# Fifty-two more tiles of an input projection formed as seven products per pair of tiles

## The chip, the cores and the metric

The kernel runs on one core of a Trainium2 chip. The metric is the device time of one execution in microseconds. TensorE (PE in the profile) multiplies matrices, and its weight loads have a row of their own (PEld); VectorE is DVE, ScalarE is ACT, GpSimd is POOL, and SyncE (SP) issues most of the DMAs.

## What is computed

The reference is one inference step of a mixer layer for 1024 prompt tokens and 8 sample tokens (1032 columns in the kernel), model width 1024, all in float32. Cut to what matters:

```
h = rmsnorm(x, norm_pre) * (1.0 + scale) + shift            # scale, shift, gate from c
proj = h @ w_in                                             # 1024 -> 10256 columns
hA, cA, bA, zA, qkv, zB, beta_raw, alpha_raw, gA, gB = split(proj)
yA = ((bA * conv3(cA * hA)) * silu(zA)) @ w_out_a           # branch A
q, k, v = split(silu(conv4(qkv)));  q, k = l2norm(q), l2norm(k)
o, S = gated_delta_chunked(q, k, v, beta, g, s0)            # 8 heads, branch B
yB = (rmsnorm(o, onorm_w) * silu(zB)) @ w_out_b
merged = sigmoid(gA) * yA + sigmoid(gB) * yB
y = x + gate * rmsnorm(merged @ w_o, norm_post)
```

The delta rule of a head works on eight chunks of 128 tokens. Per chunk c a triangular inverse U is formed, and the chunks are scanned in order: X = vp - nx * (K^T S), vn = U^T X, S = egl * S + kd^T vn, and the output of the chunk is Q^T S + DA^T vn. Convolution buffers and final states are outputs too.

## The kernel before

**Tiles and numbers.** A projection is made with 128 output columns as the stationary operand and the 1032 tokens as the moving one; one such tile is 128x1032. w_in has 80 tiles: H, C, B, Z of branch A (8 each), Q, K, V and ZB of the 8 heads (8 each), GA and GB (8 each); beta and alpha are a narrow extra tile of 48 stationary columns. Every float32 number is carried as two rounded parts (xh + xl for h, whi + wlo for a weight; ScalarE casts the high part, VectorE subtracts to get the low one), and a product is three matmuls: high x high, high x low, low x high.

**A normal tile** (`run`) goes over three groups of GW = 344 tokens, eight blocks of 128 input channels (k) and the three matmuls: 72 matmuls of 344 columns. Its weights come as one 512 KB block (`wraw`), split in two halves of 128x512.

**A pair as seven products** (`products`) takes two tiles as the columns of a 2x2 block product: the input channels in halves (weights a11, a12 for the even tile, a21, a22 for the odd one) and the tokens in halves of HT = 516. By Winograd's form of Strassen's scheme the four output blocks C11, C12, C21, C22 come from seven products P1 to P7 of half the channels by half the tokens. P1, P2, P3 and P5 use h itself or a first sum, and P6, P7, P4 and P5 use the sums T2, T3, T4 and T1 of h's quarters; weight sums are formed on VectorE. Each product has two halves of PW = 258 tokens x 4 blocks of channels x 3 matmuls, so a pair has 7 x 24 = 168 matmuls of 258 columns. In PSUM a product lies alone; `evacuate` adds it to the tiles (named acc) in SBUF.

**The order.** After the startup (h, modulation, first tile K0) `run` makes 59 tiles head by head (K, Q, V, two gates, ZB), then H, C, B, Z for t = 0 to 2 (SG = 3). At 936 us `products` makes branch A's other twenty tiles, two pairs at a time, with the sums of h written to memory (txs) and read back; `products_b` (1142 to 1224 us) makes w_out_b's eight tiles the same way; w_out_a follows as eight normal tiles (to 1320 us), and then w_o and the end (to 1420.6 us).

**What runs beside.** All else is written as generators, "strands" (`delta_gen` for a head's delta rule, `conv` strands, `gate_gen`, `weight_gen`, `block_gen` and so on). A small clock model in the kernel (`Sched`) says after each group of three matmuls (`slot`) whether a strand's last step would be finished by then with a slack (SLK = 450 ns); if so its next step is issued there. `force` steps strands until a condition holds. Queues are in order per engine, so this fixes most of the order. In `delta_gen`, DB is the strictly lower matrix of each chunk; its 32x32 diagonal blocks go to memory (sA) and come back as At, the T chain (62 small VectorE instructions on Ttmp and Tw) inverts them, the result goes through memory again (sT) and comes back as Tn, VectorE transposes it (Un), and seven TensorE steps with 32x32 and 64x64 blocks (on Qs, Tn, U, DB) build U. The scan follows with three hops per chunk:

```
stt(X, pk[:, 0:C], nx[:, c:c + 1], vp[:, c, :], ALU.mult, ALU.add)
yield
pv = ps_aux()
PE.matmul(pv[:, 0:C], lhsT=U[:, c, :], rhs=X, start=True, stop=True)
vn = bp.tile([P, C], F32, tag="vn", name="vn", bufs=2)
A.copy(out=vn, in_=pv[:, 0:C])
yield
pS = ps_aux()
PE.matmul(pS[:, 0:C], lhsT=kd[:, c, :], rhs=vn, start=True, stop=True)
```

SBUF buffers of tile width come from `Slots` (T4: NT4 = 6 equal ones, more once pools are released); PSUM has four banks for tiles (pm) and four for strands (pa). All instructions are issued through one helper, so nearly all have line L121 (L124 after the change) in the profile, and are told apart by the names of their tiles.

## Time and profile before

| | |
|---|---|
| time, median of 2 runs | 1423.52 us (1422.89 to 1424.15) |
| the profiled execution's own time | 1422.29 us |
| its span, first to last instruction | 1420.6 us |
| mean granted TensorE clock | 0.997 |
| TensorE busy | 1396.6 us (98%), 10130 instructions |
| VectorE busy | 937.7 us (66%), 2444 |
| ScalarE busy | 658.0 us (46%), 1521 |
| DMA | 161.76 MB, 114 GB/s over the span |

The profile is one execution as the hardware recorded it. Busy time counts instructions that compute; waiting, register and DMA-issuing instructions are not in it. The chain is the work that ended last, followed back from the end. A window's row gives each engine's busy time in one stretch, the clock that TensorE was granted there (1.00 is full speed), the DMA engines' busy share and what they moved.

### The profile page before, as it was taken

What the parts mean: (1) busy time and instruction counts of PE and PEld (TensorE: products, weight loads), DVE (VectorE), ACT (ScalarE), POOL (GpSimd) and SP (SyncE); (2) the same over time, 40 slices, a digit from 0 to 9 for tenths busy, and PEclk for the clock granted to TensorE, in tenths of its full rate; (3) what the DMA queues carried; (4) which work ended last, traced back from release to release, by engine and by line L of the source; (5) the groups of instructions that cost most, each with busy time, mean ns of one, the idle gap of its engine ahead of it and who ended that gap; (6) DMA issues with size and microseconds to landing.
All of it is one profiled execution on the core that took longest, in us unless ns stands there. A gap on an engine that the chain in (4) does not pass through costs nothing.

```text
span 1420.6 us, 25886 instructions
## 1 busy us (share of the span) xinstructions
PE 1396.6 (98%) x10130; PEld 1341.2 (94%) x10130; DVE 937.7 (66%) x2444; ACT 658.0 (46%) x1521; POOL 36.5 (3%) x72
## 2 busy tenths in 40 slices
PE   6999999999999999999999999999999999999997
PEld 4899999999999999999999999999999999999786
DVE  6754846758468494494764816978977857864553
ACT  6767453845529465284573332343333344532211
POOL 0000000000001000010000000000000200000000
PEclk9999999999999999999999999999999999999999
DMA  9523352233323333324232323255621875643221
GB/s 321 147 48 94 91 118 71 80 86 93 87 70 106 87 84 94 72 76 106 62 110 69 85 62 86 95 176 170 207 76 31 248 250 182 231 151 93 95 85 59
DMA packets 191396, 161.76 MB, mean 114 GB/s; under 512 B 34311, under 2 KB 166816, under 8 KB 191266
## 3 DMA queue, kind: packets, MB, share of 16 engines
q1 hardware_dynamic: 186720, 151.58, 36.3%
q0 software_dynamic: 4352, 8.46, 2.0%
q8 instruction: 79, 1.29, 0.4%
q14 instruction: 43, 0.35, 0.1%
q10 hardware_dynamic: 202, 0.08, 0.0%
HBM read 123.40 MB, written 36.91 MB: 113 GB/s over the span
## 4 chain that ended last, share of the span: by engine, by line
PE 91%; DVE 5%; DMA 3%; ACT 1%; SPq 0%; issue 0%; DVEq 0%; ACTq 0%
PE pm_t L121 66%; PE pa_t L121 22%; PE pb L121 2%; DVE kq L121 1%; DMA xs<-in_x_prompt_dram 1%; DMA yraw<-yAsc 1%; DMA wor<-in_w_o_dram 0%; DVE S L121 0%; SPq L121 0%; DMA sg<-gAsc 0%; DVE wlo L121 0%; DVE Tw L121 0%; DVE Ttmp L121 0%; DMA sg<-gBsc 0%; DVE ml L121 0%
## 5 line engine op out<-in xcount | busy, mean ns | idle before, releaser
L121 PE MATMUL pm_t<-xh,whi 128*128 128x344 f32 (+1 forms) x1576 | 520.1, 330 | 0.0
L121 PE MATMUL pm_t<-xl,whi 128*128 128x344 f32 (+1 forms) x1576 | 498.1, 316 | 0.0
L121 PE MATMUL pm_t<-xh,wlo 128*128 128x344 f32 (+1 forms) x1576 | 498.1, 316 | 0.0
L121 PEld LDWEIGHTS pm_t<-xh,whi 128*128 128x128 f32 x1576 | 297.0, 188 | 2.0
L121 PEld LDWEIGHTS pm_t<-xl,whi 128*128 128x128 f32 x1576 | 297.0, 188 | 0.2
L121 PEld LDWEIGHTS pm_t<-xh,wlo 128*128 128x128 f32 x1576 | 296.3, 188 | 0.1
L121 DVE TENSOR_TENSOR wlo<-wraw,whi 128x512 fp32r<-128x512 f32 x136 | 92.0, 687 | 49.6 <-ACT whi L121 49.3
L121 ACT CAST whi<-wraw 128x512 fp32r<-128x512 f32 x136 | 82.7, 624 | 75.9 <-PE pm_t L121 73.3
L121 ACT CAST whi<-wr 128x1024 fp32r<-128x1024 f32 x42 | 44.0, 1047 | 84.6 <-PE pm_t L121 40.7
L121 DVE SCALAR_TENSOR_TENSOR kq<-raw,vecs,kq 128x528 f32<-128x528 f32 x96 | 69.2, 761 | 1.9 <-ACT kq L121 1.9
L121 PE MATMUL pm_t<-thi,wlo 128*128 128x258 f32 x240 | 67.9, 283 | 0.1
L121 PE MATMUL pm_t<-thi,whi 128*128 128x258 f32 x240 | 67.7, 282 | 0.0
L121 PE MATMUL pm_t<-tlo,whi 128*128 128x258 f32 x240 | 67.7, 282 | 0.0
L121 PE MATMUL pa_t<-thi,whi 128*128 128x258 f32 x224 | 64.0, 286 | 1.2 <-ACT whi L121 1.2
L121 PE MATMUL pa_t<-thi,wlo 128*128 128x258 f32 x224 | 64.1, 286 | 0.8 <-DVE wlo L121 0.8
L121 PE MATMUL pa_t<-tlo,whi 128*128 128x258 f32 x224 | 63.7, 285 | 0.0
L121 PE MATMUL pm_t<-yhi,whi 128*128 128x344 f32 x192 | 61.5, 321 | 0.0
L121 PE MATMUL pm_t<-ylo,whi 128*128 128x344 f32 x192 | 61.4, 321 | 0.0
L121 PE MATMUL pm_t<-yhi,wlo 128*128 128x344 f32 x192 | 61.3, 320 | 0.0
L121 DVE TENSOR_TENSOR wlo<-wr,whi 128x1024 fp32r<-128x1024 f32 x42 | 51.2, 1219 | 14.5 <-ACT whi L121 14.5
L121 DVE TENSOR_TENSOR Ttmp<-Tw,At 128x60 f32<-128x60 f32 (+24 forms) x248 | 51.9, 209 | 8.8 <-DMA At<-sA 3.7
L121 ACT ACTIVATE junk<-pa_t 128x128 f32<-128x128 f32 x192 | 53.8, 280 | 5.6 <-PE pa_t L121 2.7
(407 smaller groups left out, 2837.2 us busy)
## 6 DMA issues: line engine op xcount, KB each, us to landing
wraw<-in_w_in_dram SPq DMA_DIRECT2D x60, 512.0 KB
wr<-in_w_in_dram SPq DMA_DIRECT2D x40, 256.0 KB
aw<-in_ada_w_dram SPq DMA_DIRECT2D x16, 512.0 KB
gBsc<-gate SPq DMA_DIRECT2D x8, 516.0 KB
gAsc<-gate SPq DMA_DIRECT2D x8, 516.0 KB
txs<-phi SPq DMA_DIRECT2D x8, 516.0 KB
txs<-plo SPq DMA_DIRECT2D x8, 516.0 KB
tlo<-txs POOLq DMA_DIRECT2D x8, 516.0 KB, 8.1
```

Source lines behind the costliest of these rows:

```text
L121: r = f(*args, **kw)
```

## The change

The tiles of x are reordered and mostly paired. Normal are K, Q and V of head 0, one gate tile, and H, C, B, Z of t = 0 (NA0 = 1): eight tiles. The other 72 are 36 pairs: H/C and B/Z of t = 1 to 7, pairs of gates, K/Q of head h, and V of head h with ZB of head h-1. Ahead of the K/Q pair of heads 1 to 7 stand 0, 2, 3, 3, 3, 3, 3 other pairs (FILL). `pairs_run` makes them one pair at a time. Products accumulate in PSUM as far as they share a sign: two tiles pp_t of two banks each ("lanes") take them, and `pair_out` moves a lane with both halves at once, 516 columns wide: four copies on ScalarE and four adds on VectorE per pair. T2, T3, T4 are made once by `block_gen`, stay in SBUF (pool tb), and T1 takes the place of the first channels' second token half in xh and xl after the last normal tile. Weights come as blocks of 128x4x128 (256 KB) in five buffers (`wr`), and splits run at most NWS = 3 products ahead in two strands (`pair_hi`, `pair_lo`).

T4 has fifteen slots of equal width; the heads' K, Q, V, kd, vp, DB, DA, At, Ts, U and gcB, which had buffers of their own, use them (Ts holds Tw, Qs, Tn and Un). Strands have ranks, a step of the lower ranks waits while VectorE or ScalarE are further than LAG1 = 2500 or LAG2 = 600 ns ahead of TensorE in the model (or HOLD = 8000 ns have gone), and the scan's slack is SLS = 200. w_out_a's tiles now come straight after the pairs, with their rows in xh and xl, and `products_b` follows them; the gates of yB are applied by halves, and the tiles of the end go in another order.

On TensorE, where head 0's inverse (on Ts, U, DB) and the start of its scan stand, the kernel before has a group of three matmuls of a normal tile (pm_t) between the steps; two pieces, the first from the inverse, the second from the scan (S,kq to X,U):

```order
L121 MATMUL pa_t<-Qs,Tn 32x32 x8
L121 MATMUL pa_t<-Tn,Qs 32x32 x8
L121 MATMUL pm_t<-xh,whi 128x344
L121 MATMUL pm_t<-xl,whi 128x344
L121 MATMUL pm_t<-xh,wlo 128x344
```

```order
L121 MATMUL pa_t<-S,kq 128x128 x2
L121 MATMUL pa_t<-qs_s,S_2391 128x2 x4
L121 MATMUL pm_t<-xh,whi 128x344
L121 MATMUL pm_t<-xl,whi 128x344
L121 MATMUL pm_t<-xh,wlo 128x344
L121 MATMUL pa_t<-X,U 128x128
```

After the change TensorE has at the same place, in the middle of pair 0 (pp_t are its lanes, T2h and T2l the parts of T2), the following rows:

```order
L124 MATMUL pp_t<-T2h,wlo 128x258
L124 MATMUL pa_t<-Ts,DB 32x32 x16
L124 MATMUL pa_t<-Ts 32x32 x24
L124 MATMUL pa_t<-U,DB 64x64 x8
L124 MATMUL pa_t<-Ts,T_728 64x64 x8
L124 MATMUL pa_t<-vp,U 128x128
L124 MATMUL pa_t<-vn,kd 128x128
L124 MATMUL pa_t<-vn,DA 128x128
L124 MATMUL pa_t<-S,K 128x128
L124 MATMUL pa_t<-S,Q 128x128
L124 MATMUL pa_t<-X,U 128x128
L124 MATMUL pp_t<-T2h,whi 128x258
```

The steps of the inverse and of the first chunk and a half now follow each other with no tile work between them, and pair 0's remaining matmuls stand behind them.

On VectorE, in the scan of head 0, the kernel before has the T chain of head 1 between the scan's rows (S and X):

```order
L121 SCALAR_TENSOR_TENSOR S_2708<-S_2651,egl_96,pa_t_2705 128x128
L121 TENSOR_TENSOR Ttmp_2498<-Tw_2497,At_2496 128x50
L121 TENSOR_TENSOR Tw_2497<-Tw_2497,Ttmp_2498 128x2x25
L121 TENSOR_TENSOR Ttmp_2498<-Tw_2497,At_2496 128x48
L121 TENSOR_TENSOR Tw_2497<-Tw_2497,Ttmp_2498 128x2x24
L121 TENSOR_TENSOR Ttmp_2498<-Tw_2497,At_2496 128x69
L121 SCALAR_TENSOR_TENSOR X_2725<-pa_t_2721,nx_1323,vp_1496 128x128
```

and after the change it has the last sums of h there (qa and qb are sums under way; T2l, T3l, T4l are low parts of the finished ones):

```order
L124 SCALAR_TENSOR_TENSOR X_1972<-pa_t_1968,nx_1364,vp_1295 128x128
L124 TENSOR_TENSOR qb_1966<-qb_1966 128x516
L124 TENSOR_TENSOR T2l_723<-qb_1966,T2h_722 128x516
L124 SCALAR_TENSOR_TENSOR S_1982<-S_1958,egl_96,pa_t_1979 128x128
L124 TENSOR_TENSOR T3l_725<-qa_1965,T3h_724 128x516
L124 SCALAR_TENSOR_TENSOR X_1993<-pa_t_1989,nx_1364,vp_1295 128x128
L124 TENSOR_TENSOR T4l_727<-qb_1966,T4h_726 128x516
L124 SCALAR_TENSOR_TENSOR S_2004<-S_1982,egl_96,pa_t_2001 128x128
```

The sums' last parts, which pair 0's own products need, stand behind rows of the scan's second to fourth step, and the scan's rows behind them.

The diff, cut to its core:

```diff
-NT4 = 6
+NT4 = 15
...
+SLS = 200.0
+LAG1, LAG2 = 2500.0, 600.0
+HOLD = 8000.0
+NWR, NWS = 5, 3
+FILL = (0, 2, 3, 3, 3, 3, 3)
+NA0 = 1
...
-SG = 3
...
+    def due(e):
+        pe = sched.clk["PE"]
+        return max(sched.clk["V"], sched.clk["A"]) <= pe + LAGS[e.pri] or e.t + HOLD <= pe
...
+    PAIRS = []
+    for h in range(1, NH):
+        for _ in range(FILL[h - 1]):
+            PAIRS.append(fill.pop(0))
+        PAIRS.append(((COL_K + h * P, 3), (COL_Q + h * P, 3), lambda a, b, h=h: (k_done(h, a), q_done(h, b))))
+        PAIRS.append(((COL_V + h * P, 3), (COL_ZB + (h - 1) * P, 0), lambda a, b, h=h: (
+            v_done(h, a), z_done(h - 1, b), start(sample_gen(h - 1)))))
...
+    EARLY = ("P4", "P1", "P2", "P6", "P5", "P7", "P3")
...
+    def pair_out(n, p, v, ta, tb):
+        pair = lambda x_: x_.rearrange("p (h n) -> p h n", h=2)
+        C11, C12, C21, C22 = (pair(x_[:, o:o + HT]) for x_ in (ta, tb) for o in (0, HT))
+        copy, adds = {"P1": (C11, ()), "P2": (None, (C11,)), "P6": (C12, ()), "P5": (C22, ()),
+                      "P7": (None, (C22, C21) if order_of(n) is EARLY else (C22,)), "P3": (None, (C12,)),
+                      "P4": (C21, ())}[p]
+        if copy is not None:
+            A.copy(out=copy, in_=v)
+        for out in adds:
+            tt(out, v, out, ALU.add)
+
+    def pairs_run():
+        for n, (e_, o_, done) in enumerate(PAIRS):
+            if n == len(PAIRS) - 2:
+                start(rows_load())
+                start(rows_split())
+            tiles, views = [], []
+            for c0, off in (e_, o_):
+                t_ = T4.take("acc", CW if off else NT, lambda: 4 if any(not h_ or flags.get(("done", h_ - 1)) for h_ in waiting) else 0)
+                if off:
+                    GP.memset(t_[:, 0:off], 0.0)
+                tiles.append(t_)
+                views.append(t_[:, off:off + NT])
+            if n % 2:
+                lanes = [ps_pair(), ps_pair()][::-1]
+            else:
+                lanes = [ps_pair(), ps_pair()]
+            for j, p in enumerate(order_of(n)):
+                blk = {"P6": "T2", "P7": "T3", "P4": "T4", "P5": "T1"}.get(p)
+                force(lambda: (n, p) in made and (blk is None or blk in blocks))
+                unit[0] = 7 * n + j
+                whi, wlo = made.pop((n, p))
+                lane = lanes[LANE.get(p, int(order_of(n) is EARLY))]
+                first = p in ("P1", "P2", "P5") or (p == "P4" and order_of(n) is EARLY)
+                for half in range(2):
+                    ps = lane[:, half, :PW]
+                    for k in range(4):
+                        xh_, xl_ = operand(p, k, half)
+                        PE.matmul(ps, lhsT=whi[:, k, :], rhs=xh_, start=first and k == 0, stop=False,
+                                  skip_group_check=True)
+                        PE.matmul(ps, lhsT=whi[:, k, :], rhs=xl_, start=False, stop=False, skip_group_check=True)
+                        PE.matmul(ps, lhsT=wlo[:, k, :], rhs=xh_, start=False, stop=k == 3, skip_group_check=True)
+                        if k < 3:
+                            slot()
+                    if half == 0:
+                        slot()
+                pair_out(n, p, lane[:, :, :PW], *views)
+                slot()
+            done(*tiles)
...
+    def block_gen():
+        part = lambda v, k: v[:, (k % 2) * HT:(k % 2) * HT + HT]
+        t1 = {}
+        for k in range(4):
+            yield from when(lambda: T4.ready(2 if k % 2 else 3))
+            a, b = T4.get("qa", NT), T4.get("qb", NT)
+            if k % 2 == 0:
+                t1[k // 2] = T4.get("q1", NT)
+            tt(a, xh[:, k, :].bitcast(F32), xl[:, k, :].bitcast(F32), ALU.add)
+            yield
+            tt(b, xh[:, 4 + k, :].bitcast(F32), xl[:, 4 + k, :].bitcast(F32), ALU.add)
+            yield
+            t_ = part(t1[k // 2], k)
+            tt(t_, a[:, HT:NT], a[:, 0:HT], ALU.subtract)
+            tt(a[:, HT:NT], b[:, HT:NT], a[:, HT:NT], ALU.subtract)
+            yield
+            tt(b[:, HT:NT], b[:, HT:NT], t_, ALU.subtract)
+            tt(b[:, 0:HT], b[:, 0:HT], b[:, HT:NT], ALU.subtract)
+            yield
+            for bl, v in (("T2", b[:, HT:NT]), ("T3", a[:, HT:NT]), ("T4", b[:, 0:HT])):
+                hi, lo = (w_[:, k, :] for w_ in T["x", bl])
+                A.copy(out=hi, in_=v)
+                yield
+                tt(lo, v, hi.bitcast(F32), ALU.subtract)
+                yield
+            T4.give(a)
+            T4.give(b)
+        for bl in ("T2", "T3", "T4"):
+            blocks[bl] = T["x", bl]
+        yield from when(lambda: flags.get("normal"))
+        for i in range(2):
+            hi, lo = (x_[:, 2 * i:2 * i + 2, HT:NT] for x_ in (xh, xl))
+            v = t1[i].rearrange("p (k n) -> p k n", k=2)
+            A.copy(out=hi, in_=v)
+            yield
+            tt(lo, v, hi.bitcast(F32), ALU.subtract)
+            T4.give(t1[i])
+            yield
+        blocks["T1"] = True
...
-    run(jobs, 1, isp)
-    products()
+    run(jobs, 1, inx)
+    flags["normal"] = True
+    pairs_run()
...
+    run(jobs, ioa, len(jobs), (ioa,))
+    RS.on = True
     products_b()
-    run(jobs, ioa, len(jobs))
```

More of the change, by code (lines that the diff above doesn't have):

```diff
@@ L719, in drain_bg @@
+            for v in held:
+                T4.give(v)
+            if after:
+                after()
+            slot()
     def drain_bg():
@@ new lines, in hybrid_step, with k_done, q_done, v_done @@
+    heads = [{} for _ in range(NH)]
+    def k_done(h, raw):
+        start(conv_gen(8 + h, raw, "K", lambda d: (heads[h].update(k=d), start(decay_gen(h, heads[h])))))
+    def q_done(h, raw):
+        start(conv_gen(h, raw, "Q", lambda d: heads[h].update(q=d)))
+    def v_done(h, raw):
+        start(conv_gen(16 + h, raw, "V", lambda d: (heads[h].update(v=d), start(delta_gen(h, heads[h])))))
+    def z_done(h, z):
+        def gen():
+            act(z, z, AF.Silu)
+            V.tensor_copy(out=z_s[:, h, :], in_=z[:, S:NT])
+            yield
+            heads[h]["sz"] = z
+        start(gen())
@@ new lines, in gate_done, with gen @@
+    def gate_done(t, sc, g):
+        def gen():
+            store(sc[t], g)
+            T4.give(g)
+            yield
+        start(gen())
+    gc_rows = lambda h: gsc.rearrange("(c h) i -> h c i", h=NH)[h].unsqueeze(0).to_broadcast([P, NC, C])
+    def decay_gen(h, st):
+        yield from when(lambda: flags.get("ba") and (not h or flags.get(("inv", h - 1))), lambda: T4.ready(2))
+        DB_, DA_ = (T4.get(n_, S) for n_ in ("DB", "DA"))
+        DB, DA = (v.rearrange("p (c i) -> p c i", i=C) for v in (DB_, DA_))
+        SY.dma_start(out=DA, in_=gc_rows(h))
@@ new lines, in hybrid_step, with pair_load, pair_split @@
+    praw = {}
+    def pair_load():
+        for n, (e_, o_, _) in enumerate(PAIRS):
+            for part in ("22", "11", "12", "21") if order_of(n) is EARLY else ("11", "12", "21", "22"):
+                c0, half = (e_, o_)[part[0] == "2"][0], int(part[1]) - 1
+                yield from when(wr_ready)
+                praw[n, part] = w_block(w_in, c0, half)
+                yield
+    def pair_split(idx, key, src):
+        yield from when(lambda: unit[0] >= idx - NWS + 1)
+        hi, lo = (wpool.tile([P, 4, P], F32R, tag=t_, name=t_, bufs=NWS) for t_ in ("whi", "wlo"))
+        A.copy(out=hi, in_=src)
+        yield
+        tt(lo, src, hi.bitcast(F32), ALU.subtract)
+        made[key] = (hi, lo)
+        yield
@@ L1471, in yblock_gen @@
             for kk in (0, 2):
+                hi, lo, give = yield from r_pair("yb", p == "P1")
                 if p in ("P1", "P2", "P3"):
[L1473 to L1474 removed]
+                    yield from when(lambda: T4.ready())
+                    raw = T4.get("yraw", NT)
                     k0 = kk if p == "P1" else 4 + kk
@@ L1671, in to_products, with gate_start @@
-    def to_products():
-        drain_bg()
+        gates_left[t] = gates_left.get(t, 2) - 1
+        if not gates_left[t]:
+            T4.give(acc_)
+    gated = {}
+    def gate_start(t, half):
+        gated[t, half] = gate_gen(t, half)
+        start(gated[t, half])
+    def products_b():
+        force(lambda: parked)
         bp.release()
         T4.extend(alloc("m", "left"), "sl", NSL, NT)
-        raw = {}
-        for g in (weight_load(raw), weight_gen(raw), block_gen()):
-            start(g)
@@ L1687, in load_rows, with rows_load, rows_split @@
+    rows = {"ya": {}}
+    yraw = {}
+    def rows_load():
         for k in range(NK):
-            yield from when(lambda: T4.ready(3))
-            raw, hi, lo = (T4.get(n_, NT) for n_ in ("yraw", "yhi", "ylo"))
-            SY.dma_start(out=raw, in_=ysc[k])
+            yield from when(lambda: T4.ready(1 + RES))
+            raw = T4.get("yraw", NT)
+            SY.dma_start(out=raw, in_=yAsc[k])
+            yraw[k] = raw
             yield
-            A.copy(out=hi.bitcast(F32R), in_=raw)
+    def rows_split():
+        for k in range(NK):
+            yield from when(lambda: k in yraw and unit[0] >= 7 * len(PAIRS) - (3 if k < 4 else 1))
+            raw = yraw.pop(k)
+            A.copy(out=xh[:, k, :], in_=raw)
@@ L1809, in prep @@
         n = P if i < 8 else NB
+        for t in range(NK):
+            finish(gated[t, 0 if 0 <= i < 4 else 1])
         xr = S_.get("xr", D)
```

941 lines of the change are left out of this document (473 added, 468 removed).

## The prediction

> **What bounds the kernel now.** I read the page first, then the windows by stage, the chain of waits, the groups by form, and the timeline where the change touches it.
>
> ```profile
> span 1420.6 us, 25886 instructions
> PE 1396.6 (98%) x10130; PEld 1341.2 (94%) x10130; DVE 937.7 (66%) x2444; ACT 658.0 (46%) x1521; POOL 36.5 (3%) x72
> PE 91%; DVE 5%; DMA 3%; ACT 1%; SPq 0%; issue 0%; DVEq 0%; ACTq 0%
> ```
>
> TensorE is busy for 98% of the span and carries 91% of the chain that ended last. So the time is TensorE's work plus the places where it stands. By stages (columns: us, then busy time of PE, PEld, DVE, ACT, POOL with instruction counts, then granted clock, DMA share, GB/s):
>
> ```profile
> 61.00:160.00 99.00, 98.22 (x645) 95.52 (x646) 58.07 (x166) 61.36 (x134) 1.38 (x5) 1.00 0.31 77
> 260.00:360.00 100.00, 99.95 (x757) 98.03 (x756) 73.12 (x227) 62.46 (x162) 3.15 (x7) 1.00 0.32 90
> 936.00:1142.00 206.00, 206.00 (x1722) 205.94 (x1722) 169.92 (x267) 73.70 (x105) 10.29 (x15) 1.00 0.52 159
> 1142.00:1224.00 82.00, 79.94 (x634) 78.28 (x633) 58.24 (x91) 37.73 (x44) 1.29 (x2) 0.98 0.62 204
> 1224.00:1320.00 96.00, 95.76 (x587) 90.99 (x586) 56.42 (x86) 32.97 (x40) 0.00 (x0) 1.00 0.48 155
> 1320.00:1420.60 100.60, 92.92 (x400) 73.73 (x398) 47.37 (x144) 18.34 (x43) 0.00 (x0) 0.98 0.20 69
> ```
>
> From 61 to 1320 us TensorE hardly stops; idle time is at the start and in the last row, which is w_o and which the change leaves nearly as it is. The third row is branch A's twenty tiles as seven products: not 0.01 us of TensorE is lost there, though VectorE works 169.92 of 206 us (82%). In the normal tiles VectorE works 59 to 73%.
>
> What the two kinds of matmul cost is in the chain (start, us, what), where a run of 48 stands without a break, since the durations of single matmuls overlap:
>
> ```profile
> 941.85 5.74 PE pm_t L121 x48
> 1239.29 7.56 PE pm_t L121 x48
> L121 PE MATMUL pm_t<-xh,whi 128*128 128x344 f32 x1416 | 474.9, 335 | 0.0
> L121 PE MATMUL pm_t<-xh,whi 128*128 128x258 f32 x160 | 45.2, 283 | 0.0
> ```
>
> The first run lies in the products: 5.74/48 = 119.6 ns for 258 columns. The second lies in w_out_a: 7.56/48 = 157.5 ns for 344. By width alone the ratio would be 0.75, and it is 0.759, so the narrow matmul loses almost nothing. The group means, 335 and 283 ns, are latencies and must not be summed.
>
> **TensorE's work: -67 us.** Before, 52 tiles of x are normal that belong to pairs afterwards (59 normal tiles and the first against 8 in all; by the instruction order 3744 matmuls of 344 go and 4368 of 258 come). A pair costs 2x72 matmuls of 344, 144 x 157.5 = 22.68 us; as seven products it costs 7x2x4x3 = 168 of 258, 168 x 119.6 = 20.09 us. 26 pairs x 2.59 = **67.3 us**. Everything else on TensorE keeps its count: head strands, w_out_a, w_out_b, w_o.
>
> Now a rule that speaks against the change. The Trainium skill, "TensorE: Matmul & The Clock Gate", section "Back-to-back issue gap", gives for streams of weight load and matmul about 81 ns at 128 columns and 131 ns at 512. Drawn straight between these (an estimate from that page) 258 columns would take 98 ns and 344 would take 109, a pair would rise from 15.7 to 16.4 us, and the 26 pairs would cost some 20 us more instead of 67 less. The two runs of 48 above contradict it: here the time grows by 37.9 ns for 86 columns, 0.44 ns a column, and not by 0.13.
>
> **Work beside it: VectorE, about +5 us.** Per pair it now has seven weight splits and four weight sums of 512, and four adds of 516 out of PSUM; ScalarE has seven casts and four copies.
>
> ```profile
> L121 DVE TENSOR_TENSOR wlo<-wraw,whi 128x512 fp32r<-128x512 f32 x136 | 92.0, 687 | 49.6 <-ACT whi L121 49.3
> L121 ACT CAST whi<-wraw 128x512 fp32r<-128x512 f32 x136 | 82.7, 624 | 75.9 <-PE pm_t L121 73.3 <-PE pa_t L121 1.8 <-ACT U L121 0.7
> L121 DVE TENSOR_TENSOR acc<-pm_t,acc 128x258 f32<-128x258 f32 x68 | 27.5, 420 | 14.9 <-PE pm_t L121 14.9
> L121 DVE SCALAR_TENSOR_TENSOR kq<-raw,vecs,kq 128x528 f32<-128x528 f32 x96 | 69.2, 761 | 1.9 <-ACT kq L121 1.9
> ```
>
> 15 instructions x 0.69 = 10.3 us a pair, against four splits (2.7 us) for two normal tiles; over 26 pairs +197 us. Against that, branch A's products before took fourteen adds of 258 per pair (the 68 of the row, and as many from the other banks, for ten pairs). With all instructions of the order priced this way VectorE goes from 1034 to 1197 us; since the page counts 937.7 where this sum gives 1034, I expect near 1086, 78% of the new span. Spread over 36 pairs it is about 20 us per 23 us of TensorE, strands included, and in some five pairs, where a head's convolution (the rows of 528) and its T chain fall together, it equals TensorE's time. Cover: splits may run two products (5.74 us) ahead, and a PSUM lane has one product of the other lane, 24 x 119.6 ns = 2.87 us, to be evacuated in; an add of 516 takes about 0.69. Lower bound 0: the window 936 to 1142 has the same ratio, 82%, and lost nothing. Upper bound: five pairs that stand 5 us each, 25. I take 5, near the row measured.
>
> **Head 0, first pair: +18 us.** This is where the order changes most. Before, head 0's inverse had 15 us to spare behind its transpose, and 344-column work between its steps:
>
> ```profile
> 135.07 0.60 DVE L121 SCALAR_TENSOR_TENSOR DB<-pa_t,cB,DB 128x128 f32<-128x128 f32 x2
> 147.67 0.19 DVE L121 TENSOR_TENSOR Ttmp<-Tw,At 128x31 f32<-128x31 f32 x1 [3.50 <-DMA At<-sA]
> 159.39 0.23 DVE L121 TENSOR_TENSOR Ttmp<-Tw,At 128x72 f32<-128x72 f32 x1
> 159.66 0.23 DVE L121 TENSOR_TENSOR Tw<-Tw,Ttmp 128x72 f32<-128x72 f32 x1
> 179.81 0.17 DVE L121 TENSOR_TENSOR Tw<-Tw,Ttmp 128x8 f32<-128x8 f32 x1
> 189.60 0.44 DVE L121 STREAM_TRANSPOSE Un<-Tn 128x256 f32<-128x256 f32 x1
> 204.51 0.69 PE L121 MATMUL pa_t<-Un,DB 32*32 32x32 f32 x16
> 205.24 0.36 ACT L121 COPY Qs<-pa_t 32x256 f32<-32x256 f32 x1 [3.22 <-PE pa_t L121]
> ```
>
> The way through memory (DB to At) takes 12 us, one T-chain instruction 0.27, the way back (Tw to Un) up to 9.8, and one step of the inverse 205.60-204.51 = 1.1. In the order of after, only some 32 us of matmuls stand between the last one that DB needs and the inverse, and TensorE's queue is in order: the rest of pair 0 stands behind the inverse, and is itself short of T2, T3, T4, whose last parts VectorE makes between the scan's steps. Working, with head 0's last DB at about 130 (its matmuls stand 5 us earlier in the order than before): At at 142; 62 T instructions of 0.2 to 0.27 (14 us) and nine large ones of 0.6 to 1.1 between them (8 us), to 164; 8 back, 172. TensorE arrives at 161 to 162: **10 us** of waiting. Behind it stand seven inverse steps (8 us) and the scan's first five chunks, with hardly one product's matmul between two hops. A hop:
>
> ```profile
> 305.67 0.38 PE L121 MATMUL pa_t<-vn,kd 128*128 128x128 f32 x2
> 306.09 0.35 DVE L121 SCALAR_TENSOR_TENSOR S<-S,egl,pa_t 128x128 f32<-128x128 f32 x1 [1.17 <-PE pa_t L121]
> 307.07 0.61 PE L121 MATMUL pa_t<-S,kq 128*128 128x128 f32 x4
> 307.49 0.35 DVE L121 SCALAR_TENSOR_TENSOR X<-pa_t,nx,vp 128x128 f32<-128x128 f32 x1 [1.05 <-PE pa_t L121]
> 308.46 0.38 PE L121 MATMUL pa_t<-X,U 128*128 128x128 f32 x2
> 308.88 0.27 ACT L121 COPY vn<-pa_t 128x128 f32<-128x128 f32 x1 [2.03 <-PE pa_t L121]
> ```
>
> 0.77, 0.77 and 0.69 us from a matmul's start to its reader's end, 2.2 a chunk and some 2.4 with the way back to TensorE: five chunks 12, the inverse 8, together 20, in a stretch whose matmuls fill 12.5: **8 us**. Bounds: 10 if the T chain comes 8 us earlier (VectorE's large rows moved less), 28 if the T blocks' last parts come late as well. I take 18. Where cover is gone, each further us on VectorE here is a us of TensorE.
>
> **The other scans: +7.** The same sum of hop needs against the matmuls that stand between, over all 64 chunks, leaves 0.6 us uncovered before and 13 after, six of them in pair 0. Nearest rows: before, 0 us are lost; with every hop bare it would be 56 chunks x about 0.5 = 28. I take 7.
>
> **Transitions: +5.** From w_out_a to w_out_b, which now change places, the row gate, the loads of yB and their splits, the first weights of w_out_b and the sums of yB crowd: about 13.5 us of VectorE by its rows beside 13.5 of TensorE. Before, the like entry cost this:
>
> ```profile
> 1142.39 8.31 DMA yraw<-yAsc
> L121 DVE TENSOR_TENSOR ylo<-yraw,yhi 128x1032 fp32r<-128x1032 f32 x8 | 9.8, 1227 | 4.8 <-ACT yhi L121 4.7
> ```
>
> The window from 1142 shows what was lost in TensorE, 82.00 - 79.94 = 2.1. Bounds 0 and 12 (the 8.31 us transfer bare, and a few splits); I take 5, with the entry to w_out_a. The end stays: the last 7.6 us have no matmul in either order. SP issues more but smaller weight loads (256 KB, twice as many), at 0.31 to 0.52 DMA share; priced at nothing, since a pair of 20 us uses four blocks, five buffers hold 25 us of work, and the longer DMA above takes 8.
>
> **Sum** against the profiled execution's own 1422.29 us (span 1420.6), 1.2 below the median of 1423.52 and inside the runs' spread of 1422.89 to 1424.15 but for 0.6: 1422.3 - 67.3 + 5 + 18 + 7 + 5 = 1390; by the median 1391. The lowest ends of the four stalls (0, 10, 0, 0) give 1365, the upper ones (25, 28, 28, 12) 1448; three of the four values lie nearer to their lower end because the nearest rows do, and I put the forecast at **1388**.
>
> **Rivals.** (a) *Nearly all of the gain arrives*: T chain early, VectorE's 82% harmless as in the products of before; only pair 0's bound of 10 is lost: 1422.3 - 67.3 + 10 = **1365**. For it: the products' 206.00 of 206.00. (b) *VectorE becomes the bound* in the pairs with heads, 25 there: with the rest as above 1355 + 25 + 18 + 7 + 5 = 1410, with the upper ends of the first pair and of the transitions too 1355 + 25 + 28 + 7 + 12 = 1427: **1410 to 1427**, taken at 1412. For it: about 87% mean load with peaks at 100%; against it, queues that even out over a pair. (c) *The slower side*: the evacuation cover of 2.87 us is missed at VectorE's adds, because a lane's next product may not start before the add that stands behind splits and strand work in VectorE's queue. Three such products a pair, 108 in all; from 0.65 us each on (a single split ahead of the add) it eats the 67 us: 108 x 0.65 = 70, **1425 and more without the other terms**, 1450 with them. Against it: the row of 258 adds shows VectorE waiting for TensorE (14.9 us idle), and no group of TensorE waiting for an add. (d) *The narrow matmul does not keep 119.6 ns* once strands and head copies stand beside it: at 135 ns a pair costs 22.68, and all the gain goes, **about 1455** with the stalls above. The skill's rule on the gap would be its reason; the row of 48 stands against it. (e) That it does not do what it says: the counts of the order exclude it.
>
> **How the numbers follow.** Forecast 0.52 (1378 to 1398), (a) 0.23 (1360 to 1378), (b) 0.19, (c) 0.04, (d) 0.02. About 2% is what a measurement of this kernel can tell from no change; 2% below the median is 1395. Faster: (a) and four fifths of the forecast's own case, 0.23 + 0.41 = 0.64. Slower by over 2% (above 1452): 0.03. Same: 0.33. The range of 8 in 10 is 1360 to 1413: it takes in (a) and the lower half of (b).
>
> **What would show it.** Right: matmul steps of 119.6 in the pairs; TensorE idle some 10 us near 162 to 172, released by a DMA of Tn or by VectorE's transpose, and in short pieces to 185; VectorE near 78%; little idle between 200 and 1200. Wrong: TensorE idle at many starts of a product behind VectorE's wlo or acc (b or c), or steps longer than 125 ns (d), or no gap near 165 (a).

## The result and the profile after

The changed kernel takes 1591.15 us (median of two runs, 1585.94 and 1596.37) against 1423.52: **11.8% slower**, ratio 1.1178, 95% interval 1.1019 to 1.1336. The forecast was 1388. The profiled execution took 1596.37 us, the slower of the two. Times are medians of a kernel's executions, without one slow execution of the first kernel under "Earlier heads". The head of its page and the chain by engine:

```profile
span 1594.7 us, 28048 instructions
PE 1427.4 (90%) x10754; PEld 1348.3 (85%) x10754; DVE 1071.9 (67%) x2625; ACT 748.1 (47%) x1655; POOL 44.5 (3%) x144
PE 53%; DVE 18%; DMA 16%; ACT 7%; issue 5%; SPq 1%; POOL 0%; DVEq 0%; ACTq 0%; POOLq 0%
```

TensorE is idle for 167 us of the span, where it was for 24. It is also busy for 31 us longer, although its matmuls should take 67 us less. The windows of after by stage (projections of x, w_out_a, w_out_b, w_o; engines as in the rows of before, then granted clock, DMA share, GB/s) show why:

```profile
61.00:1236.00 1175.00, 1077.36 (x8736) 1044.52 (x8736) 835.82 (x2145) 600.98 (x1423) 27.46 (x108) 0.94 0.29 79
1236.00:1345.00 109.00, 102.64 (x613) 97.71 (x614) 55.68 (x79) 36.96 (x44) 1.29 (x2) 0.97 0.81 265
1345.00:1458.00 113.00, 92.27 (x685) 88.06 (x683) 86.11 (x146) 46.54 (x77) 10.29 (x15) 0.92 0.65 198
1458.00:1587.00 129.00, 106.83 (x416) 79.67 (x416) 46.83 (x136) 18.82 (x44) 0.00 (x0) 0.93 0.15 51
```

The same cuts of before are these (there w_out_b stands ahead of w_out_a):

```profile
61.00:1131.00 1070.00, 1068.61 (x8117) 1048.76 (x8118) 722.53 (x2002) 518.61 (x1314) 22.69 (x35) 1.00 0.35 98
1131.00:1216.00 85.00, 82.94 (x675) 82.31 (x674) 61.55 (x98) 40.74 (x52) 7.89 (x11) 0.98 0.66 215
1216.00:1316.00 100.00, 100.00 (x622) 96.29 (x621) 60.38 (x89) 35.78 (x44) 0.00 (x0) 1.00 0.49 155
1316.00:1413.00 97.00, 96.68 (x416) 75.41 (x414) 47.45 (x137) 19.03 (x44) 0.00 (x0) 1.00 0.22 77
```

So the projections take 105 us more, w_out_b 28, w_out_a 9 and w_o 32: together the 174 us between the two spans. In the projections 98 us are idle time, and the clock of 0.94 means that it stood at half for some 140 us of the 1175, idle time included. The waits of after name the cause (engine and tile <- releaser: us in all, times, longest):

```profile
ACT DA L124 <- DMA DA<-gsc: 42.9, 8, 7.3
ACT L124 <- DMA gcB<-gsc: 34.0, 5, 9.8
ACT gcB L124 <- DMA gcB<-gsc: 12.0, 3, 5.8
PE pp_t L124 <- ACT acc L124: 38.5, 15, 8.5
PE pa_t L124 <- ACT vn L124: 19.2, 7, 5.0
PE pp_t L124 <- DVE ms L124: 15.5, 5, 8.3
ACT sqj L124 <- DMA out_dram<-yt: 30.0, 5, 6.3
```

DA and gcB are the two broadcasts of a head's decay rows, 512 KB each, 16 in all. ScalarE stands 89 us in front of them. TensorE's own largest waits, 38.5 and 19.2 us, are for two of ScalarE's copies: of a lane to acc, and of vn in the scan. Before, one load per head served both; from head 2 on it was issued 16 to 53 us before its first reader (for heads 0 and 1 only 8 and 9 us, with waits of 2.9 and 8.0). Afterwards each of the two goes into a slot of T4, and the sixteen first readers run 8.3 to 11.5 us after the issue. The timeline of after at head 1 shows one such stop from end to end (start, length, engine, operation, idle time before it):

```profile
224.30 0.37 SPq L124 DMA_DIRECT2D DA<-gsc  x1
226.72 0.28 ACT L124 ACTIVATE junk<-pa_t 128x128 f32<-128x128 f32 x1
233.68 0.40 ACT L124 ACTIVATE DA<-DA,ngc 128x128 f32<-128x128 f32 x1 [6.58 <-DMA DA<-gsc]
...
233.75 0.28 PE L124 MATMUL pp_t<-T3h,wlo 128*128 128x258 f32 x1
...
237.06 0.58 ACT L124 COPY acc<-pp_t 128x516 f32<-128x516 f32 x1
237.69 0.39 PE L124 MATMUL pp_t<-xh,whi 128*128 128x258 f32 x1 [3.65 <-ACT acc L124]
```

The load is issued at 224.30 and its first reader runs at 233.68. The copy that frees a PSUM lane (acc) stands behind it in ScalarE's queue, and TensorE waits 3.65 us for the lane. The kernel's clock model had counted 3.3 us from issue to arrival; it is 9.4. Windows of 2 us around a stop at head 2 show what follows one:

```profile
306.00:308.00 2.00, 0.39 (x4) 0.19 (x2) 0.00 (x0) 0.00 (x0) 0.00 (x0) 1.00 0.44 73
308.00:310.00 2.00, 0.00 (x0) 0.00 (x0) 0.00 (x0) 0.00 (x0) 0.00 (x0) 0.94 0.71 170
310.00:312.00 2.00, 0.00 (x0) 0.00 (x0) 0.00 (x0) 1.75 (x2) 0.00 (x0) 0.50 0.64 179
314.00:316.00 2.00, 2.00 (x11) 2.00 (x11) 1.97 (x4) 0.59 (x2) 0.00 (x0) 0.50 0.17 30
318.00:320.00 2.00, 2.00 (x19) 2.00 (x18) 1.97 (x4) 1.97 (x3) 0.00 (x0) 1.00 0.08 23
```

The last matmul ends at 306.4. The clock of 0.94 in the row from 308 to 310 places the change to half near 309.8, some 3.4 us later, and it stays there when work has come back: 11 matmuls from 314 to 316 in place of 19. The Trainium skill, "TensorE: Matmul & The Clock Gate", section "HAM oscillation — how this bites in real kernels", puts the limit at gaps of some 3.4 us. The stop at head 2 fits this, but the trace as a whole does not bear the limit out: in w_o half clock follows a stop of 2.3 us already (1533.2 to 1535.4, for ms), while stops of 1.8 and 2.0 us at 585.5 and 1326.1 have none behind them.

```profile
1533.00:1535.00 2.00, 0.15 (x1) 0.00 (x0) 0.34 (x1) 0.69 (x2) 0.00 (x0) 1.00 0.04 8
1535.00:1537.00 2.00, 1.59 (x4) 1.30 (x5) 0.41 (x2) 0.00 (x0) 0.00 (x0) 0.53 0.00 0
```

### The profile page after: what moved, and what is told of

Its sections match the earlier page's. It is cut to its first block, busy times and chain, and to the rows that moved or that the text cites. A ratio compares the mean times of both kernels' runs of the same rounds, so it can differ in the third digit from the quotient of the medians.

```text
span 1594.7 us, 28048 instructions
## 1 busy us (share of the span) xinstructions
PE 1427.4 (90%) x10754; PEld 1348.3 (85%) x10754; DVE 1071.9 (67%) x2625; ACT 748.1 (47%) x1655; POOL 44.5 (3%) x144
## 4 chain that ended last, share of the span: by engine, by line
PE 53%; DVE 18%; DMA 16%; ACT 7%; issue 5%; SPq 1%; POOL 0%; DVEq 0%; ACTq 0%; POOLq 0%
PE pp_t L124 40%; PE pa_t L124 12%; DMA DA<-gsc 4%; DMA gcB<-gsc 4%; DVE acc L124 3%; DVE wlo L124 3%; DVE Ts L124 2%; DVE Ttmp L124 2%; PE pb L124 1%; DMA sg<-gAsc 1%; ACT junk L124 1%; DVE yt L124 1%; DMA Ts<-sT 1%; ACT DA L124 1%; DVE wr L124 1%
## 5 line engine op out<-in xcount | busy, mean ns | idle before, releaser
L124 PE MATMUL pp_t<-xh,whi 128*128 128x258 f32 (+1 forms) x1624 | 493.8, 305 | 45.0 <-ACT acc L124 18.3
L124 PE MATMUL pp_t<-xl,whi 128*128 128x258 f32 (+1 forms) x1624 | 485.1, 299 | 5.9 <-DVE xl L124 5.9
L124 PE MATMUL pp_t<-xh,wlo 128*128 128x258 f32 (+1 forms) x1624 | 485.9, 300 | 1.3 <-DVE wlo L124 1.3
L124 PEld LDWEIGHTS pp_t<-xh,whi 128*128 128x128 f32 x1624 | 316.8, 195 | 55.2 <-ACT acc L124 20.7
L124 PEld LDWEIGHTS pp_t<-xl,whi 128*128 128x128 f32 x1624 | 317.0, 195 | 6.9 <-DVE xl L124 6.6
L124 PEld LDWEIGHTS pp_t<-xh,wlo 128*128 128x128 f32 x1624 | 316.6, 195 | 3.5 <-DVE wlo L124 2.7
L124 ACT CAST whi<-wr 128x512 fp32r<-128x512 f32 x250 | 153.6, 619 | 233.5 <-PE pp_t L124 192.8
L124 DVE TENSOR_TENSOR wlo<-wr,whi 128x512 fp32r<-128x512 f32 x250 | 170.3, 685 | 67.5 <-ACT whi L124 61.0
L124 DVE TENSOR_TENSOR acc<-pp_t,acc 128x516 f32<-128x516 f32 (+1 forms) x171 | 108.3, 646 | 37.6 <-PE pp_t L124 36.8
L124 ACT COPY acc<-pp_t 128x516 f32<-128x516 f32 (+2 forms) x164 | 92.0, 565 | 39.3 <-PE pp_t L124 34.0
L124 PE MATMUL pp_t<-xh,mh 128*128 128x512 f32 x128 | 55.1, 431 | 25.8 <-DVE ms L124 15.5
```

What stands on the lines that cost most here:

```text
L124: r = f(*args, **kw)
```

## The experiments

Theory A: ScalarE's queue in front of the sixteen loads, and the half clock behind each stop. Theory B: VectorE's and ScalarE's load in the pairs.

**Rows of 4 KB.** In memory the decay rows of one head lay 4 KB apart, eight rows of 512 B. Here they lie together.

```diff
+        gch = small(P, 64)
+        V.tensor_copy(out=gch.rearrange("p (h c) -> p c h", h=NH), in_=gc)
-        transpose(pt[:64, 0:C], gcf)
+        transpose(pt[:64, 0:C], gch)
...
-    gc_rows = lambda h: gsc.rearrange("(c h) i -> h c i", h=NH)[h].unsqueeze(0).to_broadcast([P, NC, C])
+    gc_rows = lambda h: gsc.rearrange("(h c) i -> h (c i)", h=NH)[h].unsqueeze(0).to_broadcast([P, S])
```

> The decay rows of all heads are stored so that one head's eight rows lie together: each of the sixteen broadcast loads (DA and gcB, 512 KB each) reads 4 KB rows in place of 512 B rows; nothing else changes, and the order of instructions stays. Theory A (ScalarE's queue stands in front of these loads, the casts and copies behind it stop TensorE, and each stop is followed by half clock): if the load takes about 3 us less, ScalarE's waits for it fall from 89 us to 40 to 50 and the time falls by 40 to 70 us, to 1520 to 1550. Theory B (VectorE's and ScalarE's load in the pairs sets the time, the waits are a symptom): within 10 us of 1591. If the load itself does not get shorter, the run tells nothing between the two.

Measured: 1504.5 us (1496.7 to 1513.9), 87 less, more than expected. The load at head 1 is now issued at 208.66 and read at 212.36, 3.7 us in place of 9.4. The DMA view of that load, first of after, then of this run:

```profile
DMA packets 1771, 0.91 MB, mean 95 GB/s; under 512 B 33, under 2 KB 1770, under 8 KB 1770
```

```profile
DMA packets 1483, 1.19 MB, mean 221 GB/s; under 512 B 48, under 2 KB 1355, under 8 KB 1483
```

The load has become 128 packets of 4 KB (1483 - 1355) in place of 1024 of 512 B. The waits, TensorE's behind ScalarE among them, and the first stage of this run:

```profile
ACT L124 <- DMA gcB<-gsc: 10.2, 5, 4.9
ACT DA L124 <- DMA DA<-gsc: 6.9, 5, 2.3
ACT gcB L124 <- DMA gcB<-gsc: 0.7, 1, 0.7
PE pp_t L124 <- ACT acc L124: 9.8, 10, 3.3
PE pa_t L124 <- ACT vn L124: 1.4, 4, 0.5
```

```profile
61.00:1138.00 1077.00, 1036.25 (x8736) 1005.09 (x8736) 835.80 (x2146) 601.05 (x1424) 27.43 (x108) 0.98 0.31 86
```

Of ScalarE's 89 us of waits 18 are left, of TensorE's 58 behind ScalarE 11; idle time falls from 98 to 41, and the clock rises to 0.98. ScalarE's and VectorE's busy time is the same to 0.1 us, so B is out as the main cause. The later stages are as long as in after (108, 112, 129 us). The shorter load also lets transfers behind it in the DMA queue come sooner: VectorE's wait for weight blocks (ws <- wr) falls from 20.2 to 12.0 us. This share of the 87 us was not measured apart.

**The model told of the latency.** In both places `sched.cur.t`, or the arrival, is raised by 7000 ns.

> The kernel's own clock model is told that each of the sixteen loads arrives 7 us later than it assumed (10 us after the issue in place of 3), so the instructions that read them are placed later in ScalarE's queue. Theory A: ScalarE's waits on these loads fall from 89 us to under 25 and the time by 60 to 120 us, to 1470 to 1530, less what the heads lose by starting later (their inverse may come bare). Theory B: within 15 us of 1591, or slower, as the heads come later.

Measured: 1549.9 (1545.9 to 1554.6), 41 less. ScalarE still waits 66 us for these loads. The waits for gcB fell from 46 to 24 us, those in front of DA hardly (42.9 to 41.8), so the edit moved DA's readers too little; why was not looked at. The loads themselves are as slow as in after, so the gain speaks for A, in part.

**No wait for the loads.** They go to a buffer in memory, and ScalarE reads `ident`.

```diff
-        SY.dma_start(out=DA, in_=gc_rows(h))
+        SY.dma_start(out=gdum, in_=gc_rows(h))
-            act(DA[:, c, :], DA[:, c, :], AF.Identity, bias=neg["gc"][:, c, h:h + 1])
+            act(DA[:, c, :], ident, AF.Identity, bias=neg["gc"][:, c, h:h + 1])
```

> The sixteen loads go to a buffer in memory that nobody reads, and ScalarE takes a constant tile in their place (the decay values are left out of the result); the same bytes are moved, and no instruction waits for them. Theory A: the 89 us of ScalarE's waits go, and with them most of TensorE's idle time between 61 and 1060 us (91 us) and of the half clock after it (53 us): the time falls by 90 to 140 us, to 1450 to 1500. Theory B: TensorE's idle time only moves to other releasers, and the time stays above 1560.

Measured: 1578.8 (1576.6 to 1582.9), only 12 less. The experiment was flawed: SyncE took from 207.8 to 248.7 us to issue five of the copies within memory, T's way out (sT) stood behind them in its queue, and head 0 waited for its own Tn (timeline):

```profile
264.16 1.70 PE L124 MATMUL pa_t<-Ts,DB 32*32 32x32 f32 x32 [41.44 <-DVE Ts L124]
```

From head 0's inverse on, which is behind this, to w_out_a it takes 958 us (264 to 1222). In after that is 1046 (190 to 1236), and with 4 KB rows 961 (177 to 1138). So from there on the heads go about as fast without these waits as with 4 KB rows.

**The same rows in the kernel before.**

> The kernel before with the 4 KB rows for its eight broadcast loads. There each load is issued long ahead of its first reader and ScalarE waits 11 us for two of them, beside matmuls that go on. Theory A says that what counts is the wait in front of other work: within 3 us of 1423.5. If the transfer's rate mattered by itself, through other transfers queued behind it, it would gain 5 us or more.

Measured: 1422.1, ratio 0.9999 (0.9989 to 1.0008). ScalarE's 11 us of waits for the load are gone, and the time is the same. The quicker load is worth nothing where nothing stands behind its reader.

**Single banks in w_o.**

```diff
-        po = [ps_main(), ps_main()]
+        po = [ps_aux(), ps_aux()]
```

> In w_o and the end the products' results go to four single PSUM banks in place of two lanes of two banks, so that a bank comes free as soon as its own half is read. Theory C (the last stage takes 139 us in place of 101 because a lane of two banks comes free only after both halves are read): 15 to 30 us less, 1561 to 1576. Rival D (the stage waits for output transfers, since its buffers are given back and taken again while the transfer runs: ScalarE waited 30 us for these): under 6 us less.

Measured: 1557.5 (1550.3 to 1561.5), 34 less. w_o takes 99 us with the clock at 0.98:

```profile
1448.00:1547.00 99.00, 98.64 (x416) 76.93 (x416) 46.45 (x136) 18.77 (x44) 0.00 (x0) 0.98 0.19 65
```

Theory C, it seems; but ScalarE still waits its 30 us for output transfers, now without harm. The converse tells more: the kernel before with two lanes in w_o.

```diff
-        po = [ps_main(), ps_main()]
+        t_ = psum["pm"].tile([P, 2, 512], F32, tag="pp", name="pp_t")
+        po = [t_[:, 0, :], t_[:, 1, :]]
```

> The converse of the run with single banks: the kernel before, whose only edit is that w_o's products go to two tiles of two PSUM banks each in place of four of one bank. If a pair of banks that comes free only as a whole is the cause of w_o's 33 us, it appears here too, without anything else of the change: 1450 to 1458. If it needs the change's fewer SBUF slots as well, less than 10 us appear.

Measured: 1428.9, 4.4 us more than 1424.55 (ratio 1.0033, 1.0020 to 1.0045). So lanes alone cost 4 us; ScalarE's waits for output transfers alone, in the run with single banks, cost nothing; both together cost the 32 to 34. Neither the kernel before nor this one has these waits. After the change fewer SBUF slots are left (21 by the kernel's constants, 35 before); what fits the waits of after is that one whose output transfer still runs is taken at once, ScalarE stops in front of it (30.0 us), and the lane that it and VectorE would have read stays taken (15.5 us of TensorE, for ms). This chain is read from the waits; slots in turn with the lanes kept was not run.

**Slots in turn, on top of both.** `Slots.get` takes the slot given back longest ago in w_o.

> On top of the 4 KB rows: w_o's products in four single banks as in the run before this one, which alone gave 33 us, and SBUF slots of the last stage taken in the order in which they were given back, so that a buffer whose output transfer still runs is not taken at once. The first part should again give 30 to 35 us (1470 to 1475); the second takes away ScalarE's 30 us of waits on output transfers and gives 5 to 10 us more (1460 to 1470) if these waits reach TensorE, and nothing if four banks already cover them.

Measured: 1475.7 (1470.1 to 1485.2), 29 under the 4 KB rows; the second part gave nothing beside the first. The executions of one of these kernels differ by 2 to 17 us. The profiled one, here the slowest of four, has stretches of half clock at heads' inverses which the run with 4 KB rows, with the same order there, does not have. These are the rows at head 7's inverse, first of the 4 KB rows, then of this run (both 9.1 of 10 us busy, clock 1.00 and 0.59):

```profile
1090.00:1100.00 10.00, 9.11 (x135) 8.46 (x134) 3.81 (x6) 7.07 (x17) 0.00 (x0) 1.00 0.31 69
1110.00:1120.00 10.00, 9.10 (x111) 8.31 (x112) 2.23 (x4) 6.39 (x15) 0.00 (x0) 0.59 0.18 57
```

**Later transfers from w_out_a on.** The first-byte time of the model, 1100, is 6000 ns there; base 4 KB rows.

> On top of the 4 KB rows: from w_out_a on, the kernel's clock model lets every transfer arrive 4.9 us later, so that ScalarE's and VectorE's instructions on loaded gates, yB and w_o rows are placed later in their queues. If w_out_b's lost time (107 us in place of 74) comes from instructions that stand in a queue before their transfer has landed, as in the heads, the stretch gets 10 to 25 us shorter: 1480 to 1495. Rival: the stretch is bound by VectorE's own load or by the transfers' rate (250 GB/s there), and the time stays within 8 us of 1504, or rises as w_o's rows come late.

Measured: 1529.2, 25 more. The blanket delay put the row gate's matmuls behind their loads in TensorE's queue (the longest stop 8.5 us), and w_out_b took 144 us. It tells nothing on the gates.

**Twelve normal tiles.** `NA0 = 2`; base 4 KB rows.

> On top of the 4 KB rows: H, C, B, Z of t = 1 are normal tiles too, so twelve normal tiles stand ahead of the pairs in place of eight. It costs TensorE two pairs' saving, 2 x 2.6 = 5 us, and gives head 0's T chain and inverse 45 us more of covered time. If the first pair's stop costs the 20 us that the trace shows (12 us idle, half clock for 24 us), the time falls by 10 to 15 us, to 1490 to 1495; if the stop only moves behind the twelve tiles, it rises by 5, to 1510.

Measured: 1549.2, 45 more, a miss. w_out_a starts 24 us earlier (1114), yet takes 169 us, since work of the heads was left for it. Head 0's stop did not go; it became 10.9 us. The model sets the inverse where it believes the data to be, which the run with later round trips below bears out:

```profile
172.61 1.69 PE L124 MATMUL pa_t<-Ts,DB 32*32 32x32 f32 x32 [10.92 <-DVE Ts L124]
```

**VectorE's load.** Base for this and the next three: 1475.7 us. Three weight sums per pair are left out.

> Base for all four runs: 4 KB rows, single banks and slots in turn in w_o (1475.7 us). Here three of the four weight sums per pair are left out (products of unsummed blocks, so the result is not the reference's): VectorE does 3 x 36 instructions of 0.6 us less, 65 us of its work in the pairs. If VectorE's load holds TensorE in the pairs (theory B), the time falls by 20 us or more; if what is left there are waits for round trips and hops, by less than 8.

Measured: 1472.7 (1470.6 to 1474.2): 3 us of the whole for 65 us of VectorE's work. But the parts moved. The projections, w_out_a and w_out_b of the base's profile, then of this one:

```profile
61.00:1161.00 1100.00, 1055.21 (x8737) 1023.17 (x8736) 836.41 (x2146) 602.72 (x1424) 27.33 (x108) 0.96 0.30 84
1161.00:1269.00 108.00, 102.89 (x615) 98.08 (x616) 55.24 (x80) 36.32 (x43) 1.75 (x3) 0.97 0.80 266
1269.00:1378.00 109.00, 92.40 (x683) 88.14 (x682) 80.83 (x138) 44.08 (x74) 9.81 (x14) 0.91 0.62 192
```

```profile
61.00:1118.00 1057.00, 1022.46 (x8667) 996.97 (x8668) 770.16 (x2012) 591.47 (x1389) 27.49 (x108) 0.98 0.30 85
1118.00:1244.00 126.00, 114.63 (x678) 106.55 (x679) 63.80 (x105) 43.21 (x76) 1.03 (x2) 0.96 0.71 234
1244.00:1365.00 121.00, 98.39 (x688) 89.90 (x687) 81.97 (x137) 47.05 (x77) 10.58 (x15) 0.89 0.61 187
```

The projections are 43 us shorter than in the base's profile (its slowest execution) and 20 shorter than with 4 KB rows alone, the two behind them together 30 longer, with some 70 matmuls more. So the run does not rule VectorE's load out as a cost in the pairs; it shows that the whole gains only 3 us from lifting it.

**The scan's slack.** `SLS = 450.0`.

> The scan's slack is 450 ns, as before the change, in place of 200: each hop's next matmul is placed a quarter of a us later. If bare hops cost what the order suggested (some 7 us outside the first pair), the time falls by 5 to 10 us; if the later end of each head pushes work into w_out_a, it rises by 5 to 20.

Measured: 1476.0 (1474.1 to 1484.3). No change of the whole; here too the parts moved, 30 us off the base's projections (1070) and 21 more behind them (238 for 217).

**The round trips.** `t_at`, and the time behind the load of Tn, are 5000 ns later.

> The clock model is told that the T chain's two ways through memory (At, and the way back to Tn) take 5 us longer than it assumed. Same theory as for the decay rows: instructions stood in a queue before their data. TensorE waits 12 us for Ts and 11 for ScalarE's acc behind it; if that is this cause, the time falls by 10 to 20 us plus the half clock behind it; if head 0's inverse only moves to where still less covers it, it stays within 8.

Measured: 1465.1 (1454.0 to 1468.4), 11 less. TensorE's wait for Ts falls from 11.7 to 1.0 us. The stages of its profile, which is its fastest execution (1454.0):

```profile
61.00:1113.00 1052.00, 1019.22 (x8662) 993.45 (x8662) 824.31 (x2117) 592.10 (x1388) 27.17 (x108) 0.99 0.30 86
1113.00:1229.00 116.00, 109.00 (x684) 102.56 (x684) 60.74 (x103) 44.73 (x79) 1.22 (x2) 1.00 0.71 239
1229.00:1347.00 118.00, 93.72 (x688) 88.79 (x688) 87.55 (x144) 43.98 (x76) 10.38 (x15) 0.88 0.67 208
```

In this execution the projections are 18 us shorter than before the change, but 74 small matmuls fewer stand in them than in after (8662 for 8736): the last head ends later, inside w_out_a. w_out_a and w_out_b together take 49 us more than before the change.

**Gates and w_o's rows later.** 5000 ns on these two loads.

> In w_out_b's stretch the clock model is told that the gates of yB and w_o's rows arrive 5 us later, and of no other transfer. VectorE waited there for ScalarE's sigmoid (4.8 us) and cast (4.6 us), behind these transfers, with the adds that free PSUM banks queued behind. If that is the cause of the stretch's 16 us of idle time and 7 of half clock, the time falls by 8 to 20 us; if the crowd of transfers (250 GB/s) is, by less than 4.

Measured: 1472.6 (1471.0 to 1473.0), 3 less: under what was expected. In the profiles w_out_b is 8 us shorter (101 for 109) and w_o 9 longer (106 for 97), which suggests that these loads are part of that stretch's loss.

**Earlier heads.** Base for the rest: 1465.1 us. `FILL = (0, 2, 2, 2, 2, 2, 2)`, then `(0, 2, 2, 2, 3, 3, 3)`, then `(0, 2, 2, 2, 2, 3, 3)` with the later gates.

> Base: 4 KB rows, w_o's banks and slots, and the later round trips (1465.1 us). Two other pairs ahead of every head from the third on, in place of three (FILL 0, 2, 2, 2, 2, 2, 2), so head 7 ends some 80 us before w_out_a in place of inside it. If w_out_a's and w_out_b's lost time comes from head 7's late end (its output is stored 42 us after w_out_a's start, and row gate, yB's blocks and sums crowd behind it), the stretch from w_out_a's start to w_o's gets 25 to 45 us shorter (234 us now) and the whole 15 to 40, less what tighter heads cost: 1425 to 1450. If the order of the two projections itself or its transfers is the cause, the stretch stays within 8 us.

> The same with FILL (0, 2, 2, 2, 3, 3, 3): head 7 ends some 35 us before w_out_a. By the theory of the late head about half of the gain of FILL 2 throughout: 1440 to 1458; it tells how much of a loss in the heads the tighter setting brings.

> FILL (0, 2, 2, 2, 2, 3, 3) together with the gates and w_o's rows placed later: between the two others, less some 3 us: 1432 to 1452. It is to show whether the parts add up and how near the version with pairs comes to the time before (1423.5).

Measured: 1528.4, 1491.8 and 1502.6: all slower. From w_out_a's start to w_o it takes 226, 225 and 225 us, against 233 in the base's profile, so the late head is not the cause there; that theory fell. The projections took 1121 us with FILL 2 (idle 56, clock 0.96), 69 more than the base:

```profile
61.00:1182.00 1121.00, 1065.09 (x8752) 1025.82 (x8752) 837.61 (x2150) 603.20 (x1423) 30.11 (x108) 0.96 0.30 84
```

Heads that follow each other faster leave less tile work between their steps. That this is what costs far more than the stretch behind gains is argued from the idle time and the clock; no run sets it apart.

**What holds w_out_b.** `start(wo_gen())` moved behind `products_b()`; and, apart from it, the gate of yB left out.

> Base: the 1465.1 us kernel. w_o's rows are loaded and split only after w_out_b in place of beside it. If they crowd w_out_b's stretch (118 us in place of 82 of matmuls), the stretch gets 8 to 20 us shorter, and the start of w_o waits some 20 us for them in turn; if the stretch stays within 4 us, they are not its cause.

> Base: the 1465.1 us kernel. The gate of yB is left out in w_out_b's stretch (no load of gB, no sigmoid, no product with it; the sum with yA's part stays, so the outputs lack this gate). It takes 16 loads, 16 ScalarE and 16 VectorE instructions of half tiles away. If VectorE's waits for them, ahead of the adds that free banks, cause the stretch's loss, it gets 10 to 25 us shorter (1440 to 1455); if the start (yB's first blocks, 14.7 us) and yB's splits are the cause, by less than 8.

Measured: 1462.4 (1458.9 to 1469.1), w_out_b 121 us: w_o's rows are not its cause. Without the gate 1449.7 (1445.2 to 1454.3), 15 less, w_out_b 105 us in place of 118:

```profile
1243.00:1348.00 105.00, 88.47 (x687) 84.91 (x686) 78.75 (x129) 37.78 (x61) 10.07 (x15) 0.93 0.67 206
```

By one profile of each, some 13 of the 33 us that w_out_b takes more than before the change are the gates: the additions of the two branches, which stood beside w_out_a before, now stand here with them. What is left is mostly its start, a stop of 14 us in this run as in its base (timeline of the base): TensorE waits for yB's first blocks, behind their load. This stop came with the later round trips, which put head 7's end later: it is 3.0 us in after and 5.0 in the 1475.7 us kernel.

```profile
1249.87 1.05 ACT L124 CAST xh<-yraw 128x1032 fp32r<-128x1032 f32 x1 [17.91 <-DMA yraw<-yBsc]
1250.97 0.80 PE L124 MATMUL pp_t<-xh,whi 128*128 128x258 f32 x2 [14.71 <-ACT xh L124]
```

No version tried beats the kernel before.

## Why the prediction was wrong, step by step

**TensorE's work, -67: right, as far as the profiles tell.** TensorE has 624 matmuls more (10754 for 10130), which is 4368 less 3744. In after a run of 47 matmuls in a pair stands in the chain with 120 ns each:

```profile
1144.83 5.64 PE pp_t L124 x47
```

In the 1465 us kernel the projections are 18 us shorter than before, with 31 us more of idle time (1052 - 1019 against 1070 - 1069) and, by the clock of 0.99, some 11 us lost to it: 18 + 31 + 11 = 60 us of work saved, by this rough account. For after itself it gives 96 us more idle time and 70 lost to the clock, less the 105 that the projections take longer: 61. The clock is given to 0.01, which is 10 to 12 us.

**Loads at nothing: the step that failed.** The prediction priced SP's issues by the weight loads alone, took 8 us as the longest transfer, and found buffers enough. It did not list DA's and gcB's loads, although they move from a buffer filled far ahead into slots filled just before use. Such a load takes 9 us, ScalarE's queue stands in front of it, and the copies that free PSUM lanes stand behind. Their rows of 512 B cost 87 us, half clock included.

**Half clock: no term at all.** Each stop was priced by its own length, but the rows at head 2 and in w_o show half clock behind stops of 6.7 and of 2.3 us. In after, idle time in the projections is 98 us and the clock took up to 70 more.

**First pair, +18: about right, by luck.** With 4 KB rows TensorE stops 5.7 us for Ts, not 10, and the inverse and scan then run for 24 us at half clock, which costs up to 12: the sum is near, but its larger part was not in the forecast. The windows of that run show that a chain of small matmuls does not bring the clock back:

```profile
178.00:180.00 2.00, 1.31 (x27) 1.21 (x26) 0.00 (x0) 1.57 (x5) 0.00 (x0) 0.50 0.03 8
182.00:184.00 2.00, 1.73 (x16) 1.76 (x16) 0.00 (x0) 0.12 (x1) 0.00 (x0) 0.50 0.00 0
```

**VectorE, +5, and the scans, +7: not much larger than forecast.** VectorE is busy for 1071.9 us, where some 1086 were forecast, and in the projections of after TensorE waits 4.6 us for its acc and 3.8 for its wlo. For the scan's vn TensorE waits 19.2 us in after, but 1.4 with 4 KB rows, so that wait came from ScalarE's queue and not from bare hops. 65 us less of VectorE gave the whole 3 us, more slack in the scan nothing; the parts that moved in these two runs leave open what either costs in the pairs.

**Transitions, +5: too small.** w_out_b and w_out_a lose 37 us (28 and 9). The gates' work was not in the sum, and the wait for yB only in its upper bound of 12; in after TensorE waits 9.6 us in w_out_b for yB's blocks and sums (xh, xl), 5.0 for VectorE's acc and 4.7 for the first operand of w_o (mh), and the clock there is 0.92. The row that priced the entry, the 8.31 us load of yAsc, belongs to w_out_a's rows inside w_out_b's stretch, not to its start: w_out_b runs from 1131 to 1216 us before the change and w_out_a to 1316, not from 1142 to 1224 and to 1320.

**The end unchanged: wrong.** The last 7.6 us are, but w_o in front of them takes 32 us more; the PSUM lanes and the smaller number of slots there were not looked at, and the runs with single banks and with lanes in the kernel before show that it takes both.

**The rivals.** (c), the slower one, named the right symptom, a lane freed late, but by VectorE's adds. It was ScalarE's copy, behind a transfer. No rival had a transfer at the head of a queue. The sum of (c) with the other terms is 1455, where it says 1450. Of the forecast's own signs, those against (b), (c) and (d) held: little idle time behind wlo and behind VectorE's acc (5.1 and 9.7 us in the whole span), and 120 ns a matmul. But "little idle between 200 and 1200" did not: TensorE is idle for 71 us there.

## What to carry to other kernels

When buffers are shared to make room, list every load that goes into them, and compare issue and first reader before and after; a reader placed 6 us too early in an in-order queue stops all that stands behind it, here the copies that free PSUM. Price a stop of TensorE of more than some 2 us at its length and some microseconds of half clock more. A model that places instructions must have the measured time of each kind of transfer, 9.4 us here for one that it held for 3.3.
